# A hybrid encoder layer on one core: the second token group's feature-major products as seven quarter products, the lanes beside token-major blocks, an output block in two depth halves

## The chip, the cores and the metric

The kernel runs on one core of a Trainium2 chip. The metric is device time in microseconds (us), from the first to the last instruction of the core. TensorE (PE) multiplies matrices into PSUM, VectorE (DVE) and ScalarE (ACT) do elementwise work, GpSimd (POOL) does a little of it, and the SyncE queue (SP) issues the transfers.

## The reference, cut to what matters

One encoder layer is applied to 1024 + 256 tokens of width 2048, with shared weights, in fp32. The normalised input is multiplied by `w_in`, and the product's columns go to three groups of heads, whose results are concatenated and multiplied by `w_out`:

```python
proj = rms_norm(x, norm_g) @ w_in                    # 2048 x 4896
xbc, z_ssd, dt_raw, q, k, v, z_att, mq, z_mem = split_cols(proj, IN_SIZES)
xbc = silu(centred_dwconv(xbc, conv_w, conv_b))      # 1536 columns, 5 taps over tokens
o_ssd = rms_norm((scan(xbc, dt) + scan_back(xbc, dt) + skip) * silu(z_ssd))
o_att = window_attention(q, k, v, sink) * silu(z_att)
o_mem = softmax(mq @ mk) @ mv * silu(z_mem)          # mk, mv from the memory tokens
y = x + concat([o_ssd, o_att, o_mem]) @ w_out        # 2048 x 2048
```

## The kernel before, in words

The ten tiles of 128 tokens are two groups of five: tokens 0 to 639 (group one, `grp` 0) and 640 to 1279 (group two, `grp` 1). Every fp32 operand is split into a high part (`h`, ScalarE) and the remainder (`l`, VectorE), so that each product is three matmuls: h·h, h·l, l·h. For weights this is `wsplit` (L200 to L204), one ScalarE and one VectorE instruction per depth step; `wh` and `wl` have three buffers each (`WB`), so weights are split up to three depth steps ahead of TensorE. A group's input rows lie in SBUF as `xH`, `xL` in four quads of four depth steps.

There are three kinds of product blocks.

- `block_tok` (L230): token-major. Sixteen depth steps, each with five token tiles times three matmuls of 512 columns (288 for "kv"). Used for the memory blocks, "q", "kv", "mq", "z0", "z1" and, for the first 640 output tokens, the four output blocks `o`.
- `block_feat` (L264): feature-major. 256 features by 640 tokens in two halves of 320: 2 x 2 x 16 depth steps x 3 = 192 matmuls of 320 columns. Group two uses it for the ten units x0 to x5 (the convolution's input), za0, za1, zm0, zm1 (gates).
- `block_pair` (L1174): the same 256 x 640 unit by seven quarter products of half depth instead of eight, from sums and differences of rows (`tH`, `tL`) and of weights (`weight_sums`, L1154, four POOL instructions per depth step): 7 x 8 x 3 = 168 matmuls of 320 columns. Group one uses it for its ten units, `rows_in` picking the operands; the output for group two uses it at the end (8 units). Its evacuation is `ev_seven` (L1271), whose units' partial sums lie in a tile with the tag `xst`. Statistics (`stage_stats`, L1356) load pieces of the inputs into the same tag.

What follows a convolution unit (five taps, tanh, product: L345 to L379) or a gate unit is put into the queue `left` and issued piece by piece by `some_left`. `p_step` (L1260) builds group one's rows by a written plan: load, scale by the norm (`p_fill`, L1227, with the splits), sums (`p_sums`), splits of the sums (`p_split`).

The rest runs in two **lanes**, queues of generators that are stepped beside the blocks: lane 0 has the key preparation, attention `attn` and memory attention `mem_attn`; lane 1 has the scans' preparation `dt_prep`, `ssd_up` and `ssd_down`. `run` (L1361) calls `pump(rates)` once per depth step; `RATES` gives how many steps of lane 0 and lane 1 fall due then, by block. `need(fn, ts)` steps a lane until the named generators are done. The framework that builds the kernel keeps each lane's order but places an instruction in its engine's order where its inputs are expected, so lane matmuls come to lie between block matmuls.

The order before: two memory blocks and "q" of group one; ten units of quarter products of group one; then, with the lanes beside them, "kv", "mq", "z0", "z1" of group one, x0 to x4, "kv", x5, "q", za0, za1, "z0", "z1", "mq", zm0, zm1 of group two, output blocks o0, o1 and the first nine steps of o2; the rest of o2 and o3 with `beside_step`, which builds the rows of the output's quarter products; those eight units.

All loads and stores are issued by the SP queue.

Of the kernel before, what the change touches and what calls it, by code (L numbers as in the profile page):

```python
# [19 lines left out]
P = 128  # L20
# [23 lines left out]
def hymba_encoder_kernel(  # L44
# [65 lines left out]
    k_d = [dram([P, P], f"k_{t}") for t in range(NT)]  # L110
# [119 lines left out]
    def block_tok(w, nt, evac, before_last=None, feats=range(KT), places=range(KT)):  # L230

        load, n = w
        ps = [acc.tile([P, 512], F32, tag="acc", name="acc") for _ in range(nt)]
        hls = {}
        for k in range(KT):
# [7 lines left out]
            if k == KT - 2:  # L243
                continue
            if k == KT - 1 and before_last is not None:
                before_last(k)

            for t in range(nt):
                for k_ in ((k - 1, k) if k == KT - 1 else (k,)):
# [6 lines left out]
                    T.matmul(ps[t][:, :n], sl, h[:, :n], start=False, stop=(k_ == KT - 1))  # L256
                if k == KT - 1:
                    with tc.high_priority(offset=HP[0]):
                        evac(t, ps[t])
            if k == KT - 1:  # L260
                yield k - 1
# [64 lines left out]
    def ev_dtkv(base):  # L326
        def f(i, ps):
            t = base + i
            r = ev.tile([P, P], F32, tag="evt" if i % 2 else "evu", name="kraw")
            A.activation(r, ps[:, 32:160], AF.Copy)  # L330
            S.dma_start(k_d[t], r)
            V.tensor_add(dt_all[:, t, :], ps[:, :32], dtb)
            V.tensor_copy(v_all[:, i + (2 if base else 0), :], ps[:, 160:288])
        return f
# [63 lines left out]
    def ev_out(c0):  # L398
        def f(t, ps):
# [5 lines left out]
            S.dma_start(yt, xrow(t)[:, c0:c0 + 512])  # L405
            V.tensor_add(yt, ps, yt)
            S.dma_start(y_first[t * P:(t + 1) * P, c0:c0 + 512], yt)
# [68 lines left out]
    def k_prep(t):  # L476
        r = w2("kr")[:, :P]
        S.dma_start(r, k_d[t])
# [8 lines left out]
        r3 = hv(r, 2)  # L487
        V.tensor_mul(r3, r3, hb(rr, 2, 64))
# [19 lines left out]
    def kv_shift():  # L508

        V.tensor_copy(kT[:, :, 0:2 * P], kT[:, :, 3 * P:5 * P].bitcast(F32))  # L510
        V.tensor_copy(kL[:, :, 0:2 * P], kL[:, :, 3 * P:5 * P].bitcast(F32))
        V.tensor_copy(v_all[:, 0:2, :], v_all[:, 3:5, :])

    def dt_prep(t0):
# [6 lines left out]
        x = flat(dt_all)  # L521
        e, s = [mp.tile([P, 512], F32, tag="xs", name=n, bufs=2)[:, :160] for n in "es"]
# [275 lines left out]
    def ssd_up(t):  # L798
# [63 lines left out]
        for g in range(2):  # L862
# [23 lines left out]
            if not last:  # L886
                ps = psum("pst")
                into(ps, g, fh, fl)
                if t == 0 and g == 0:

                    need(mk_prep, range(4))
# [328 lines left out]
    def p_load(k):  # L1220

        raw[k] = [rp.tile([P, 640], F32, tag="ch", name=n, bufs=CH) for n in ("ra", "rb_")]
        for i in range(2):
            r = k + 8 * i
            S.dma_start(raw[k][i], x_turned[0, r * P:(r + 1) * P, :])

    def p_fill(k):  # L1227

        for i, x in enumerate(raw[k]):
            q, j = divmod(k + 8 * i, 4)  # L1230
            if j == 0:
                new_quad(q)
            g_ = R_G + k + 8 * i
            V.scalar_tensor_tensor(out=x, in0=x, scalar=vec[:, g_:g_ + 1], in1=rbc, op0=ALU.mult, op1=ALU.mult)
            h, l = cur["H", q][:, j, :], cur["L", q][:, j, :]
            A.activation(h, x, AF.Copy)
            V.tensor_sub(l, x, h.bitcast(F32))

# [32 lines left out]
    def ev_seven(kind, f0):  # L1271

        work, o = (conv_left, 2) if kind is None else (gate_left, 0)

        def begin(u):
            if kind is None:
                tiles = [rp.tile([P, 650], F32, tag="ch", name="u", bufs=CH) for _ in range(2)]
                for x in tiles:
                    V.memset(x[:, :2], 0.0)
            else:  # L1280
                tiles = [ev.tile([P, 650], F32, tag="evu", name="r") for _ in range(2)]
            r0, r1 = [hv(x[:, o:o + 640], 2) for x in tiles]
            w = None

            def f(p, ps):
# [10 lines left out]
                elif p == 3:  # L1296
                    V.tensor_add(r0[:, 1], ps, w[:, 1])
# [139 lines left out]
    def vectors(_):  # L1437
# [6 lines left out]
        for _ in range(4):  # L1444
            yield
# [235 lines left out]
```

## Time and profile before

| what | value |
|---|---|
| median of three runs | 1803.67 us (1800.71 to 1803.76) |
| the profiled execution: its time | 1800.71 us |
| its span | 1800.7 us |
| granted TensorE clock | 1.000 |
| HBM read, written | 231.12 MB, 57.44 MB |
| 16 DMA engines' share of the first queue | 52.7% |

A row of a stretch gives its bounds, its length, then for each engine the busy time and the number of instructions, the granted clock, the share of the DMA engines and what they moved. A row of a group gives line, engine, operation, tiles and shapes, the count, then busy time in us and the mean duration in ns, then the idle time ahead of it and what ended that. A row in order of time begins with the start and the duration in us.

### The profile page before, as it was taken

How to read it: one execution, taken by the hardware profiler on the slowest of the kernel's cores; microseconds unless marked ns; L12 is line 12 of the kernel's file. 1: busy time of each engine (PE TensorE's matmuls, PEld its weight loads, DVE VectorE, ACT ScalarE, POOL GpSimd, SP SyncE). 2: the span in 40 equal slices, each digit the busy share in tenths (PEclk: the TensorE clock that was granted, in tenths of full speed). 3: DMA queues.
4: the chain of work that ended last, by engine and by line, in shares of the span. 5: the costliest groups of instructions: out<-in, count | busy, mean ns of one | idle time of the engine just before them, and what ended most of it. 6: DMA issues, size and time to landing. Idle time of an engine off the chain costs nothing.

```text
span 1800.7 us, 30423 instructions
## 1 busy us (share of the span) xinstructions
PE 1791.2 (99%) x10546; PEld 1606.1 (89%) x10546; DVE 1244.3 (69%) x2422; ACT 903.0 (50%) x2039; POOL 439.5 (24%) x714
## 2 busy tenths in 40 slices
PE   9999999999999999999999999999999999999999
PEld 7789999999887899999989987887898888889999
DVE  5595788877657978775755866666885654866665
ACT  6554455444445756564435646544574533543332
POOL 0105789961110000000000000001100000058775
PEclk9999999999999999999999999999999999999999
DMA  8664455446544644444436355457785564644442
GB/s 291 198 179 120 138 153 146 129 136 218 164 136 147 184 134 140 121 132 134 119 96 192 110 161 180 128 178 235 231 266 168 184 190 138 216 153 147 142 143 80
DMA packets 198891, 290.58 MB, mean 161 GB/s; under 512 B 18960, under 2 KB 80464, under 8 KB 198736
## 3 DMA queue, kind: packets, MB, share of 16 engines
q1 hardware_dynamic: 198592, 288.57, 52.7%
q8 instruction: 83, 1.36, 0.3%
q14 instruction: 72, 0.59, 0.1%
q10 hardware_dynamic: 144, 0.06, 0.0%
HBM read 231.12 MB, written 57.44 MB: 160 GB/s over the span
## 4 chain that ended last, share of the span: by engine, by line
PE 61%; DVE 1%; ACT 1%; issue 1%; DMA 1%; POOL 0%; POOLq 0%; ACTq 0%; DVEq 0%
PE acc L254 9%; PE acc L256 8%; PE acc L255 8%; PE acc L289 5%; PE acc L291 5%; PE acc L290 5%; PE acc L1199 3%; PE acc L1201 3%; PE acc L1200 3%; PE py L931 2%; PE po L674 1%; PE ppt L664 1%; PE accm L1200 1%; PE accm L1201 1%; PE accm L1199 1%
## 5 line engine op out<-in xcount | busy, mean ns | idle before, releaser
L203 DVE TENSOR_TENSOR wl<-wraw,wh 128x512 fp32r<-128x512 f32 (+1 forms) x480 | 338.9, 708 | 241.3 <-ACT wh L202 230.7
L254 PE MATMUL acc<-wh,xH 128*128 128x512 f32 (+1 forms) x1248 | 481.9, 386 | 0.2 <-ACT mkr L416 0.2
L255 PE MATMUL acc<-wl,xH 128*128 128x512 f32 (+1 forms) x1248 | 472.2, 378 | 0.9 <-DVE wl L203 0.6
L256 PE MATMUL acc<-wh,xL 128*128 128x512 f32 (+1 forms) x1248 | 472.8, 379 | 0.0
L202 ACT ACTIVATE wh<-wraw 128x512 fp32r<-128x512 f32 (+1 forms) x480 | 292.4, 613 | 323.5 <-PE acc L256 173.3
L254 PEld LDWEIGHTS acc<-wh,xH 128*128 128x128 f32 x1248 | 234.5, 188 | 45.1 <-issue 4.8
L255 PEld LDWEIGHTS acc<-wl,xH 128*128 128x128 f32 x1248 | 234.7, 188 | 43.8 <-DVE wl L203 3.3
L256 PEld LDWEIGHTS acc<-wh,xL 128*128 128x128 f32 x1248 | 234.2, 188 | 43.9 <-issue 0.9
L289 PE MATMUL acc<-xH,wh 128*128 128x320 f32 x640 | 204.5, 320 | 0.0
L291 PE MATMUL acc<-xH,wl 128*128 128x320 f32 x640 | 198.6, 310 | 0.0
L290 PE MATMUL acc<-xL,wh 128*128 128x320 f32 x640 | 198.3, 310 | 0.0
L203 DVE TENSOR_TENSOR sl<-ws,sh 128x384 fp32r<-128x384 f32 x144 | 99.6, 695 | 96.9 <-ACT sh L202 96.6
L202 ACT ACTIVATE sh<-ws 128x384 fp32r<-128x384 f32 x144 | 74.6, 523 | 176.5 <-POOL ws L1171 81.5
L1171 POOL TENSOR_TENSOR ws<-wraw 128x128 f32<-128x128 f32 x144 | 91.1, 633 | 202.0 <-DMA wraw<-in_w_in_pairs_dram 83.6
L289 PEld LDWEIGHTS acc<-xH,wh 128*128 128x128 f32 x640 | 120.3, 188 | 4.1 <-issue 3.7
L290 PEld LDWEIGHTS acc<-xL,wh 128*128 128x128 f32 x640 | 120.3, 188 | 2.6 <-issue 2.2
L291 PEld LDWEIGHTS acc<-xH,wl 128*128 128x128 f32 x640 | 120.1, 188 | 0.7 <-issue 0.6
L1171 POOL TENSOR_TENSOR ws<-wraw,ws 128x128 f32<-128x128 f32 x144 | 93.5, 649 | 11.3
L358 DVE SCALAR_TENSOR_TENSOR c<-u,vec,c 128x638 f32<-128x638 f32 (+1 forms) x96 | 88.6, 926 | 10.0 <-ACT c L353 9.7
L1171 POOL TENSOR_TENSOR ws<-ws,wraw 128x128 f32<-128x128 f32 x144 | 94.2, 654 | 0.0
L120 POOL TENSOR_SCALAR qr<-qss 128x8 f32<-128x8 f32 x10 | 4.3, 428 | 366.6 <-DVE qss L598 366.6
L1171 POOL TENSOR_TENSOR wraw<-wraw 128x128 f32<-128x128 f32 x144 | 89.2, 620 | 11.1
(427 smaller groups left out, 3645.1 us busy)
## 6 DMA issues: line engine op xcount, KB each, us to landing
wraw<-in_w_in_laid_dram SPq DMA_DIRECT2D x208, 256.0 KB, 2.8
wraw<-in_w_in_pairs_dram SPq DMA_DIRECT2D x80, 256.0 KB, 2.8
wraw<-in_w_out_laid_dram SPq DMA_DIRECT2D x64, 256.0 KB, 3.5
wraw<-in_w_out_pairs_dram SPq DMA_DIRECT2D x64, 256.0 KB, 2.8
rf<-ac SPq DMA_DIRECT2D x40, 256.0 KB, 3.7
rb<-ac SPq DMA_DIRECT2D x40, 256.0 KB, 4.1
wraw<-in_w_mem_laid_dram SPq DMA_DIRECT2D x32, 256.0 KB, 4.8
xst<-in_x_sample_dram SPq DMA_DIRECT2D x20, 256.0 KB, 4.7
```

The costliest lines, as they stand in the source:

```text
L202: a = A.activation(h, raw, AF.Copy)
L203: b = V.tensor_sub(l, raw, h.bitcast(F32))
L254: T.matmul(ps[t][:, :n], sh, h[:, :n], start=(k_ == 0), stop=False)
L255: T.matmul(ps[t][:, :n], sh, l[:, :n], start=False, stop=False)
L256: T.matmul(ps[t][:, :n], sl, h[:, :n], start=False, stop=(k_ == KT - 1))
L289: T.matmul(o, sh, cur["H", q][:, m, c], start=(k == 0), stop=False)
L290: T.matmul(o, sh, cur["L", q][:, m, c], start=False, stop=False)
L291: T.matmul(o, sl, cur["H", q][:, m, c], start=False, stop=(k == KT - 1))
L358: V.scalar_tensor_tensor(out=c[0], in0=u[:, k:k + n], scalar=cw[k], in1=c[0], op0=ALU.mult, op1=ALU.add)
L1171: G.tensor_tensor(out=o, in0=x, in1=y, op=op)
L1199: T.matmul(ps[p], h, xh, start=(k_ == 0), stop=False)
L1200: T.matmul(ps[p], h, xl, start=False, stop=False)
```

## The change

Group two's ten feature-major units become quarter products too, ahead of the lanes. "kv" and "mq" of group one run before them without lanes, and beside these two blocks `t_step` builds group two's rows; the scaled rows of both groups are kept in DRAM (`xs_d`) and read back. The lanes then run beside seven token-major blocks: "kv", "q", "mq", "z0", "z1" of group two, and, with group one's rows read back, "z0", "z1" of group one. The four token-major output blocks are cut in depth: the first half (attention and memory attention) with the lanes, its sums with `x` added parked in DRAM (`ym_d`); the second half (scans) after it, added to the parked sums. `RATES` are higher, as the lanes have fewer depth steps. "kv" is written to DRAM whole and read back by the lanes. The statistics of tokens 640 to 1279 move ahead, in the first quarter-product stretch, with a fifth step per unit.

```diff
-RATES = ({'kv': (2.0, 1.0), 'mq': (2.4, 1.6), 'z0': (2.2, 1.7), 'z1': (2.2, 1.7)},
-         {'kv': (1.2, 1.5), 'x': (1.75, 1.85), 'q': (1.6, 2.5), 'za': (1.6, 2.5), 'z0': (1.55, 2.6),
-          'z1': (1.55, 2.65), 'mq': (1.55, 2.8), 'zm': (1.55, 2.85), 'o': (1.95, 1.9)})
+RATES = {'kv': (2.0, 2.0), 'q': (3.1, 3.3), 'mq': (3.1, 3.3), 'z1': (3.1, 3.3), 'z0': (3.1, 3.3), 'o': (3.1, 3.6)}
...
-            S.dma_start(yt, xrow(t)[:, c0:c0 + 512])
+            S.dma_start(yt, ym_d[c][t] if part else xrow(t)[:, c0:c0 + 512])
             V.tensor_add(yt, ps, yt)
-            S.dma_start(y_first[t * P:(t + 1) * P, c0:c0 + 512], yt)
+            S.dma_start(y_first[t * P:(t + 1) * P, c0:c0 + 512] if part else ym_d[c][t], yt)
...
+    def p_scale(k, grp=0):
 
         for i, x in enumerate(raw[k]):
+            r = k + 8 * i
+            V.scalar_tensor_tensor(out=x, in0=x, scalar=vec[:, R_G + r:R_G + r + 1], in1=rbc, op0=ALU.mult, op1=ALU.mult)
+            S.dma_start(xs_d[grp][r], x)
...
+    def r_load(k):
+
+        again[k] = [rp.tile([P, 640], F32, tag="ch", name=n, bufs=CH) for n in ("ra", "rb_")]
+        for i in range(2):
+            S.dma_start(again[k][i], xs_d[1][k + 8 * i])
+
+    def r_fill(k):
+        p_rows(k, again.pop(k))
...
+    t_plan = {}
+    for k in range(8):
+        at = (3, 6, 9, 12, 15, 17, 19, 21)[k]
+        for j, f in ((at - 2, lambda k: p_load(k, 1)), (at, lambda k: p_scale(k, 1)), (at + 1, p_sums), (at + 2, p_split)):
+            t_plan.setdefault(j, []).append((f, k))
+    for k, at in enumerate((25, 27, 29, 31, 32, 33, 35, 37)):
+        for j, f in ((at - 2, r_load), (at, r_fill)):
+            t_plan.setdefault(j, []).append((f, k))
...
+    def pairs_in(grp, extra):
+        nonlocal owe
+        for u, unit in enumerate(units):
+            for k in block_pair(w_in_pairs, u, rows_in, ev_seven(*unit, grp), lead=2):
+                if k in (0, 2, 4, 5, 7):
+                    next(squares, None)
...
+    pairs_in(0, p_step)
...
+    run(block_tok(w_in_rows("kv"), 5, ev_dtkv(0)), (0, 0), extra=left_and(t_step))
+    run(block_tok(w_in_rows("mq"), 5, ev_raw(mq_d, 0), feats=PAIRED, places=PAIRED), (0, 0),
+        extra=left_and(lambda k: t_step(16 + k)))
+    pairs_in(1, t_step)
     early.close()
...
+    def first_steps(k):
+        while left and k > 2:
             some_left()
 
+    tok("kv", 1, ev_dtkv(5), extra=first_steps, hold=4)
...
+    tok("q", 1, ev_raw(q_d, 5))
+    tok("mq", 1, ev_raw(mq_d, 5))
+    tok("z0", 1, ev_gate(0, 5))
+    tok("z1", 1, ev_gate(1, 5), refill_x(0))
+    tok("z0", 0, ev_gate(0, 0))
...
+    tok("z1", 0, ev_gate(1, 0), lambda q: refill_o(0)(q) if q < 2 else [])
...
+    for c in range(4):
+        run(block_tok(w_out_rows(c), 5, ev_out(c, 0), feats=range(8), places=range(8)), RATES["o"],
+            (lambda q: refill_o(0)(q + 2)) if c == 2 else None)
+    for c in range(4):
+        j0 = 8 * c - 16
+        rest = range(8, KT)
+        for k in block_tok(w_out_rows(c), 5, ev_out(c, 1), before_last=lambda _: beside_step(j0 + 6), feats=rest, places=rest):
...
             if j0 + k < -7:
-                pump(RATES[1]["o"])
+                pump(RATES["o"])
```

More of the change, by code (lines that the diff above doesn't have):

```diff
@@ L487, in k_prep @@
         r3 = hv(r, 2)
+        need(vectors, [0])
         V.tensor_mul(r3, r3, hb(rr, 2, 64))
@@ L1282, in begin @@
             r0, r1 = [hv(x[:, o:o + 640], 2) for x in tiles]
+            second = ((0, 64, 324), (64, 320, 392)) if kind is None and grp else ((0, 320, o + 320),)
             w = None
@@ L1566, in hymba_encoder_kernel @@
+    queue(0, attn, range(5, 10))
     queue(1, dt_prep, [5])
[L1567 to L1576 removed]
+    queue(1, ssd_up, range(4, 8))
```

229 lines of the change are left out of this document (112 added, 117 removed).

## The prediction, made before the changed kernel was run

> **What bounds the kernel now.** I read the page's busy shares first, then the busy time by stretch, then the order of time of TensorE and VectorE.
>
> ```profile
> span 1800.7 us, 30423 instructions
> PE 1791.2 (99%) x10546; PEld 1606.1 (89%) x10546; DVE 1244.3 (69%) x2422; ACT 903.0 (50%) x2039; POOL 439.5 (24%) x714
> ```
>
> TensorE is idle for 9.5 us of 1800.7. A busy matmul is modelled and may be waiting, so I checked the distance from start to start. Three places follow: the quarter products of the first group, a feature-major block of the second, a token-major block. Each pair of lines is the first and the last of a run of matmuls with nothing else between them.
>
> ```profile
> 379.81 0.31 PE L1201 MATMUL acc<-xH,sl 128*128 128x320 f32 x1
> ...
> 387.99 0.30 PE L1200 MATMUL acc<-tL,sh 128*128 128x320 f32 x1
> ...
> 639.76 0.31 PE L290 MATMUL acc<-xL,wh 128*128 128x320 f32 x1
> ...
> 642.99 0.31 PE L291 MATMUL acc<-xH,wl 128*128 128x320 f32 x1
> ...
> 499.65 0.39 PE L254 MATMUL acc<-wh,xH 128*128 128x512 f32 x1
> ...
> 502.85 0.39 PE L256 MATMUL acc<-wh,xL 128*128 128x512 f32 x1
> ```
>
> 57 matmuls, 23 matmuls and 15 matmuls stand there: 8.18/56 = 0.146 us, 3.23/22 = 0.147 us and 3.20/14 = 0.229 us each. Duration (0.31, 0.39) is not cost; spacing is. VectorE is read the same way; its order of time has a weight split, and what came next:
>
> ```profile
> 607.14 0.68 DVE L203 TENSOR_TENSOR wl<-wraw,wh 128x512 fp32r<-128x512 f32 x1
> 607.74 0.94 DVE L637 TENSOR_REDUCE m<-lg 128x2 f32<-128x768 f32 x1
> ```
>
> The next one starts 0.60 us after a start whose duration is 0.68: 0.08 us of each duration is overlap. Now the stretches: the quarter products of group one, the first "kv", the first "z1", the first "zm" up to the output, block "q" of group one with the building of its rows, and all in which the lanes run.
>
> ```profile
> core 0: us, PE busy (x) PEld busy (x) DVE busy (x) ACT busy (x) POOL busy (x), PEclk, DMA share, GB/s
> 151.90:399.20 247.30, 246.85 (x1681) 245.47 (x1680) 197.00 (x298) 126.25 (x253) 201.95 (x310) 1.00 0.47 138
> 399.20:430.80 31.60, 31.60 (x242) 31.60 (x241) 21.55 (x49) 16.70 (x43) 4.17 (x10) 1.00 0.78 242
> 553.10:632.50 79.40, 79.22 (x410) 62.33 (x408) 72.57 (x165) 54.43 (x142) 3.67 (x4) 1.00 0.55 164
> 1258.70:1335.70 77.00, 76.55 (x518) 70.68 (x517) 64.33 (x151) 45.61 (x116) 6.53 (x14) 1.00 0.81 251
> ...
> 96.80:151.90 55.10, 54.99 (x241) 44.90 (x241) 44.10 (x72) 26.82 (x45) 11.36 (x20) 1.00 0.53 160
> ...
> 399.20:1544.80 1145.60, 1142.75 (x6641) 997.28 (x6640) 784.43 (x1702) 592.87 (x1458) 68.13 (x108) 1.00 0.54 164
> ```
>
> The reader is to see two things. The 1680 matmuls of the quarter products take 247.3 us, 0.147 us each, so that stretch has no slack to lose or to win. And in the lane stretch the granted clock is 1.00 and VectorE is busy 0.68 of the time, but 0.91 in "z1" (72.57 of 79.40) while TensorE misses 0.18 us. TensorE bounds every stretch; only fewer matmuls shorten it.
>
> **The change, part by part.**
>
> **Fewer products.** These rows of the page go.
>
> ```profile
> L289 PE MATMUL acc<-xH,wh 128*128 128x320 f32 x640 | 204.5, 320 | 0.0
> L291 PE MATMUL acc<-xH,wl 128*128 128x320 f32 x640 | 198.6, 310 | 0.0
> L290 PE MATMUL acc<-xL,wh 128*128 128x320 f32 x640 | 198.3, 310 | 0.0
> ```
>
> 1920 matmuls leave, 1680 come (ten units of seven products, eight depth steps, three matmuls): 240 fewer at 0.147 us is **-35.3 us**. All other matmuls keep their number and width; the output block in halves has 8 x 5 x 3 twice instead of 16 x 5 x 3 once.
>
> **The second quarter-product stretch.** It repeats 151.90:399.20 with the same POOL sums. The convolution taps come with it. They cost more beside POOL than in the lane stretch, by the mean:
>
> ```profile
> L358 DVE SCALAR_TENSOR_TENSOR c<-u,vec,c 128x638 f32<-128x638 f32 x37 | 36.6, 991 | 0.1
> ```
>
> against 887 ns (row below). But the first stretch carried these very taps with TensorE 246.85 of 247.30 busy, so I take 0; if the cover went, the 48 taps' 0.1 us each are 5 us.
>
> In the first stretch a wait is added: the statistics get a fifth step per unit and their pieces share one buffer (`xst`) with the units' sums, so that in seven of ten units a piece is alive when the sums begin. Behind the first sum stand the unit's six others on VectorE, and the next unit's first product needs the bank.
>
> ```profile
> xst<-in_x_sample_dram SPq DMA_DIRECT2D x20, 256.0 KB, 4.7
> ```
>
> A piece that starts only then lands 4.7 us later; the 42 matmuls of the last two depth steps take 6.1 us. It fits by a little; I take 0, with 7 x 1 us as the other end.
>
> **Rows of group two, built beside "kv" and "mq".** Without lanes, the matmuls there take 31.6 + 54.5 = 86 us. The same work for group one has these prices:
>
> ```profile
> L1234 DVE SCALAR_TENSOR_TENSOR ra<-ra,vec,rbc 128x640 f32<-128x640 f32 x8 | 7.0, 879 | 0.0
> L1237 DVE TENSOR_TENSOR xL<-ra,xH 128x640 fp32r<-128x640 f32 x8 | 6.5, 818 | 0.0
> L1243 DVE TENSOR_TENSOR ra<-ra 128x320 f32<-128x320 f32 x8 | 4.1, 517 | 0.0
> ```
>
> 16 scalings, 32 subtractions and 24 splits of rows (eight more fall into the first product unit), 14 left-over taps, 16 narrow and 16 wide weight splits (0.458 and 0.688, rows below), each less the 0.08: 13 + 14 + 18 + 11 + 6 + 10 = 72 us of 86, a share of 0.84. Block "q" did such work at 44.10 of 55.10, 0.80, and TensorE missed 0.11 us. I take 0; should the cover fail, it is the 3 us or so by which 0.84 exceeds 0.80. The 48 added transfers of 0.33 MB are 16 MB, spread over "kv", "mq", "q" and the block ahead of it, some 190 us: 84 GB/s on top of the 160 of "q" is less than the 251 of "zm", so 0 for them too.
>
> **The lane stretch.** The two lanes (attention, memory attention, state scans) move from 1145.6 us to behind the second product stretch, beside seven token-major blocks and the output halves. TensorE first. Of the 1145.6 us, the wide token-major blocks are 10 x 240 x 0.227, "kv" 2 x 240 x 0.132, the feature-major ones 1920 x 0.147: 545 + 63 + 282 = 890. (0.227 is what most pairs of neighbours show, 54.5 us per block and within 1% of the 0.229 above; 0.132 is 31.60/240.) The rest, 255 us and some, is the lanes' own matmuls with every wait in it. Afterwards: one "kv" 32, six blocks 327, four half blocks 109, nine steps of 15 matmuls 31, and the same 255: **754 us**. The rates drain the lanes there: 12 steps at 2.0, 96 at 3.1, 41 at 3.1 make 449 for lane 0, whose generators have 442 steps; 24 + 96 x 3.3 + 41 x 3.6 = 488 for lane 1 with 487. The scans that the third half block's refill needs are step 396, and 409 are then done. So nothing is forced at the end.
>
> VectorE next. What leaves its 784.4 us, with the rows:
>
> ```profile
> L203 DVE TENSOR_TENSOR wl<-wraw,wh 128x512 fp32r<-128x512 f32 x241 | 165.6, 688 | 163.8 <-ACT wh L202 154.7 <-DMA rb<-ac 3.5 <-DMA xc<-xbc_d 2.7
> L358 DVE SCALAR_TENSOR_TENSOR c<-u,vec,c 128x646 f32<-128x646 f32 x48 | 42.3, 887 | 9.8 <-ACT c L353 9.7
> L203 DVE TENSOR_TENSOR wl<-wraw,wh 128x288 fp32r<-128x288 f32 x31 | 14.2, 458 | 23.9 <-ACT wh L202 23.9
> L190 DVE SCALAR_TENSOR_TENSOR chd<-chd,vec,rbc 128x640 f32<-128x640 f32 x16 | 13.8, 880 | 0.4 <-DMA chd<-in_x_turned_dram 0.4
> L364 DVE SCALAR_TENSOR_TENSOR u<-u,c 128x646 f32<-128x646 f32 x12 | 9.9, 827 | 0.2 <-ACT u L361 0.2
> L358 DVE SCALAR_TENSOR_TENSOR c<-u,vec,c 128x638 f32<-128x638 f32 x11 | 9.7, 879 | 0.1
> L406 DVE TENSOR_TENSOR yt<-acc,yt 128x512 f32<-128x512 f32 x14 | 9.5, 686 | 2.2 <-PE acc L256 2.1
> L315 DVE SCALAR_TENSOR_TENSOR zs<-zs,acc 128x320 f32<-128x320 f32 x16 | 7.4, 484 | 5.1 <-ACT zs L314 5.1
> ...
> L202 ACT ACTIVATE wh<-wraw 128x512 fp32r<-128x512 f32 (+1 forms) x480 | 292.4, 613 | 323.5 <-PE acc L256 173.3
> ```
>
> 104 wide splits of 0.688 (137 of 241 stay), 15 narrow ones, 48 taps and 12 last steps, 16 scalings, 16 gate products: 71.6 + 6.9 + 52.2 + 13.8 + 7.4 = 152. Eleven more output additions of 0.686 come: +8. So 784 - 152 + 8 = **640 us in 754, a share of 0.85**, below the 0.91 that "z1" bears with 0.18 us of TensorE idle. ScalarE has 593 less 104 splits of 0.61 (the last row), some 530 of 754. Transfers: 164 GB/s x 1145.6 us = 188 MB, less 104 x 0.26 MB and with 5 MB of parked halves 166 MB, 220 GB/s; "zm" had 251. None is over a level that the trace shows without loss.
>
> **The price of density.** The trace has no place with 6.4 lane steps in a depth step; "z1" has 3.9 in 79.40/16 = 5.0 us. What a lane's wait costs is seen there: a score matmul, the end of its softmax, and its transposes.
>
> ```profile
> 600.80 0.41 PE L632 MATMUL psc<-kT,qT 128*128 128x384 f32 x1
> ...
> 610.01 0.74 DVE L652 TENSOR_SCALAR lg<-lg,den 128x384 f32<-128x384 f32 x2
> ...
> 610.48 0.88 PE L664 MATMUL ppt<-identr,lg 128*128 128x128 f32 x6
> ```
>
> The chain lasts 9.7 us and TensorE fills it with block matmuls: the transposes stand in its order where their input is ready, between two matmuls of one triple. So density alone costs near nothing as long as block matmuls are at hand. The dearest known spot is the start: 14 left-over convolution steps are issued at once in the fourth step of "kv" (11 taps of 0.88 and 3 last steps of about 0.82, less the 0.08: 11 us of VectorE), while TensorE has split weights for three steps of 31.60/16 = 2.0 us. 11 - 6 is 5 us; with 1 us for four more block changes **+6**. Its ends are 0 (the same left-overs beside the first "kv", one per step, cost nothing: 31.60 busy of 31.60) and 19, the whole burst with the 1 us and the 7 us of the statistics.
>
> **Sum.** 1800.7 - 35.3 + 6 = 1771.4 for the profiled execution. It was the fastest of the three runs shown, its time 1800.71 being its span; the median is 3.0 higher: **1774 us**.
>
> **Rivals.**
>
> **VectorE becomes the bound.** I took 0.08 us of each duration as overlap. If each instruction held the engine for all of it, the 640 us would grow by 0.08 for each of some 1702 - 200 instructions: 120 us, 760 in all, more than TensorE's 754. With no idle time that is +6; with the 0.09 that VectorE still idles in "z1" it is 760/0.91 = 835, +81. The start-to-start row lies at the lower end, so I take +35 of this band, from its lower half: 1800.7 - 35.3 + 35 + 3 = 1803, no change. The spacing row speaks against it. [...]
>
> **TensorE waits at the lanes' turns (slower).** Place: the 40 groups of transposes of attention and the 20 of memory attention. Score and transpose are three lane-0 steps apart; at 3.1 steps in 754/149 = 5.1 us that is 4.9 us against a chain of 9.7. If the order cannot put enough block matmuls between, because only three depth steps of weights are split ahead, each group waits. Longest waits now:
>
> ```profile
> PE pmt L759 <- DVE mpr L751: 1.3, 2, 0.8
> PE ppt L664 <- DVE lg L652: 0.9, 2, 0.5
> ```
>
> It decides from 35.3/60 = 0.6 us per group; at 0.8 it is 48 us: 1800.7 - 35.3 + 48 + 3 = 1816. For it speaks the density, against it that these four waits came to 2.2 us in the whole stretch.
>
> **The saving is not there**, because the product stretch is bound by something else: excluded by 0.147 us per matmul in both forms.
>
> **How the numbers follow.** Forecast 1774, its own band 1762 to 1790: 0.64. VectorE bound, 1790 to 1810: 0.18. Waits at the turns, 1807 to 1850: 0.15. Better than 1762: 0.03. This kernel's measurement tells 0.2% (3.6 us) from no change, so "same" is 1800 to 1807. Of the second case I put 0.06 below, 0.08 in and 0.04 above it: faster 0.73, same 0.08, slower 0.19. The range 1762 to 1806 leaves out 0.03 below and some 0.17 above.
>
> **What would show it.** Right: 1680 more matmuls on the lines of the quarter products (4704 with the output's) and none on the feature-major lines; two stretches of about 247 us; a lane stretch of 754 to 765 us with VectorE busy 0.83 to 0.87 and the waits of TensorE under 10 us in all; "kv" of group two near 37 us plus its lane matmuls. Wrong: VectorE over 0.95 there and TensorE's matmuls waiting for `wl`; or waits of `ppt` and `pmt` of over 30 us; or a second product stretch over 255 us.

## The result, and the profile after

The changed kernel takes **1825.92 us** (median of 4, 1822.18 to 1831.61), the kernel before 1802.34 us (1800.71 to 1803.76): a ratio of **1.0136 [1.0121, 1.0152]**, slower by 24 us where the prediction had it faster by 30. The profiled execution after took 1827.37 us with a span of 1825.6.

The head of the page of after, the same two lines that the prediction quotes of before:

```profile
span 1825.6 us, 31134 instructions
PE 1779.5 (97%) x10306; PEld 1575.4 (86%) x10306; DVE 1394.0 (76%) x2638; ACT 952.9 (52%) x2117; POOL 654.1 (36%) x1034
```

10306 matmuls against 10546: the 240 are gone. But TensorE is now idle for 46.1 us (1825.6 - 1779.5), before for 9.5. Where that is, the busy times by stretch of after show: "q" of group one; the first quarter products; "kv" and "mq" of group one, with group two's rows built beside them; the second quarter products; all the rest up to the end of the second closing half block, with the lanes.

```profile
core 0: us, PE busy (x) PEld busy (x) DVE busy (x) ACT busy (x) POOL busy (x), PEclk, DMA share, GB/s
98.40:159.20 60.80, 56.89 (x242) 45.81 (x240) 45.80 (x75) 27.60 (x46) 10.96 (x20) 0.97 0.63 213
159.20:413.50 254.30, 249.41 (x1690) 246.54 (x1689) 196.91 (x303) 131.65 (x269) 201.88 (x314) 1.00 0.46 142
413.50:509.00 95.50, 90.39 (x484) 78.29 (x483) 77.52 (x125) 40.35 (x70) 17.11 (x24) 0.96 0.77 252
509.00:755.60 246.60, 245.78 (x1681) 245.40 (x1680) 205.02 (x331) 116.69 (x205) 198.39 (x296) 1.00 0.36 112
755.60:1569.30 813.70, 790.26 (x4230) 640.22 (x4229) 649.92 (x1454) 481.08 (x1244) 68.63 (x104) 0.99 0.62 196
```

Against what the same work took or should take:

| Stretch | after, us | basis, us | excess |
|---|---|---|---|
| start of the kernel to the first quarter product | 159.2 | 151.9 (before) | 7.3 |
| first quarter products | 254.3 | 247.3 (before) | 7.0 |
| "kv", "mq" of group one | 95.5 | 86.3 (31.6 and 54.5, and the change of block) | 9.2 |
| second quarter products | 246.6 | 247.3 (forecast) | -0.7 |
| lane stretch | 813.7 | 777.8 | 35.9 |

The basis of the last row is the forecast's 754 us with the seven steps of the second closing half block that it left out, 7 x 15 x 0.227 = 23.8. The excesses add up to 58.7 us (59.4 less the 0.7), of which the forecast had 6. The saving of 35 us is there, and more than one and a half times as much is spent. In the lane stretch 23.4 us of the 35.9 are idle time of TensorE (813.70 - 790.26); 6.8 us more are its clock, shown below, and the other 5.7 us stand in no row of idle time. VectorE is busy 649.9 us, 0.80, not at its limit (682.7 us in 816.15, 0.84, in a run below). In "kv" and "mq" 5.1 us of the 9.2 are idle time, and 3.4 the clock.

The waits of TensorE in that stretch of after (engine, what it wanted, who ended the wait, then us in total, times, longest):

```profile
PE ppt L674 <- DVE lg L662: 7.2, 3, 3.4
PE pms L747 <- ACT mqh L732: 3.2, 2, 2.7
PE pacs L563 <- DVE w L552: 2.7, 2, 1.4
PE pst L867 <- ACT fh L881: 1.5, 3, 0.8
PE acc L255 <- ACT wh L202: 1.3, 1, 1.3
PE pst L867 <- ACT bh L894: 1.3, 1, 1.3
```

No place stands out: 23 waits in all, most for a lane's own data, two (2.0 us) for a block's weights. The longest can be followed. First the load that it began with, in the view of the tile `yd` between 1276 and 1283 us: its data was stored by `ssd_up` from 1273.0 on, the load was issued at 1276.5 and landed 5.1 us later, at 1281.6.

```profile
L1018 SPq DMA_DIRECT2D yd<-yp x1: 326/326/326, 1276.5 to 1276.5; - x1
...
DMA to landing us min/median/max: 5.1/5.1/5.1
```

Then the order of time of after around it, VectorE, ScalarE and TensorE (start, duration, engine, instruction, in brackets the idle time before it and what ended that):

```profile
1278.53 0.15 DVE L650 TENSOR_TENSOR m<-m,sinkb 128x2 f32<-128x2 f32 x1
1281.74 0.69 DVE L1040 TENSOR_TENSOR yd<-yd,zd 128x512 f32<-128x512 f32 x1 [3.05 <-issue]
1282.35 0.16 DVE L651 TENSOR_SCALAR nm<-m 128x2 f32<-128x2 f32 x1
...
1282.47 0.63 ACT L1041 ACTIVATE zd<-yd 128x512 f32<-128x512 f32 x1 [6.91 <-DVE yd L1040]
...
1283.19 0.60 ACT L657 ACTIVATE lg<-lg,nm 128x384 f32<-128x384 f32 x1
...
1282.92 0.39 PE L255 MATMUL acc<-wh,xH 128*128 128x512 f32 x1
1286.73 1.05 PE L674 MATMUL ppt<-identr,lg 128*128 128x128 f32 x6 [3.42 <-DVE lg L662]
1287.43 0.67 PE L642 MATMUL psc<-kT,qT 128*128 128x384 f32 x1
```

Read it from the top. A product of lane 1 waits 3.05 us on VectorE; the profile names no releaser (`issue`), but the product starts as the load lands. Behind it stands `nm` of lane 0's softmax, whose input was there at 1278.7 and which runs at 1282.35: VectorE ran its instructions in their order. Behind `nm` on ScalarE are the exponentials, which also stand behind lane 1's square. (VectorE then waits another 1.02 us for lane 1's `yrs`, ahead of the softmax's `den`.) The transposes of that softmax stand in TensorE's order ahead of the other 14 matmuls of the block's depth step, whose weights were split by 1275.8: these could have run. A lane that is late for 3 us thus stops the other lane and then TensorE for 3.4 us. And it doesn't end there; the busy times of after in the 3.35 us that follow:

```profile
1287.35:1290.70 3.35, 3.35 (x12) 2.96 (x11) 1.86 (x6) 1.91 (x6) 0.00 (x0) 0.50 0.74 233
```

The granted clock is 0.50, and block matmuls of 512 columns start 0.43 us apart in place of 0.227. Before had no such window in its span; in the lane stretch of after there are four of 3.4 us, each behind 3.4 us in which TensorE was idle for 2.0 to 2.9, which costs another 4 x 1.7 = 6.8 us.

### The profile page after: what moved, and what is told of

Its sections match the earlier page's. It is cut to its first block, busy times and chain, and to the rows that moved or that the text cites. A ratio compares the mean times of both kernels' runs of the same rounds, so it can differ in the third digit from the quotient of the medians.

```text
span 1825.6 us, 31134 instructions
## 1 busy us (share of the span) xinstructions
PE 1779.5 (97%) x10306; PEld 1575.4 (86%) x10306; DVE 1394.0 (76%) x2638; ACT 952.9 (52%) x2117; POOL 654.1 (36%) x1034
## 4 chain that ended last, share of the span: by engine, by line
PE 73%; DMA 9%; issue 7%; DVE 6%; POOL 3%; ACT 2%; SPq 0%; ACTq 0%; POOLq 0%; DVEq 0%
PE acc L256 9%; PE acc L257 9%; PE acc L255 9%; PE acc L1208 8%; PE acc L1206 8%; PE acc L1207 8%; PE accm L1207 3%; PE accm L1206 3%; PE accm L1208 3%; PE py L938 2%; POOL ws L1178 1%; DVE wl L203 1%; PE po L684 1%; PE ppt L674 1%; PE pyb L1036 1%
## 5 line engine op out<-in xcount | busy, mean ns | idle before, releaser
L1178 POOL TENSOR_TENSOR ws<-wraw,ws 128x128 f32<-128x128 f32 x224 | 150.7, 673 | 17.3
L1178 POOL TENSOR_TENSOR ws<-ws,wraw 128x128 f32<-128x128 f32 x224 | 151.4, 676 | 0.0
L1208 PE MATMUL acc<-xH,wl 128*128 128x320 f32 x320 | 98.9, 309 | 3.2 <-DVE wl L203 3.2
L1206 PE MATMUL acc<-xH,wh 128*128 128x320 f32 x320 | 99.1, 310 | 1.7 <-ACT wh L202 1.7
L1207 PE MATMUL accm<-tL,wh 128*128 128x320 f32 x320 | 99.0, 310 | 0.0
L1206 PE MATMUL accm<-tH,wh 128*128 128x320 f32 x320 | 99.0, 309 | 0.0
L1208 PE MATMUL acc<-tH,sl 128*128 128x320 f32 x320 | 98.9, 309 | 0.0
L1207 PE MATMUL acc<-xL,wh 128*128 128x320 f32 x320 | 98.7, 308 | 0.0
L1206 PE MATMUL acc<-tH,sh 128*128 128x320 f32 x320 | 98.6, 308 | 0.0
L1208 PE MATMUL accm<-tH,wl 128*128 128x320 f32 x320 | 98.5, 308 | 0.0
```

The costliest lines, as they stand in the source:

```text
L1178: G.tensor_tensor(out=o, in0=x, in1=y, op=op)
L1206: T.matmul(ps[p], h, xh, start=(k_ == 0), stop=False)
L1207: T.matmul(ps[p], h, xl, start=False, stop=False)
L1208: T.matmul(ps[p], l, xh, start=False, stop=(k_ == 7))
```

## The experiments

Two theories at the start. **Density**: the lanes' chains are as long as before, but there are fewer block matmuls to put between their steps, and engines that run their instructions in order, as VectorE did above, pass each delay on. **VectorE**: more work per us on it makes it the bound, the prediction's first rival. Each stretch with an excess then got its own runs. Where kernels were profiled again with a stretch untouched, its length moved: "q" 58 to 63 us, the first quarter products 251 to 258, the lane stretch 814 to 818.

### VectorE with more work, and with less

More: a clearing of 320 columns of `rbc`, which nothing reads any more, at each of 149 depth steps. (A tile of its own to clear did not fit into SBUF: 57 kb of a partition, where 56.1 are left.)

```
     def pump(rates):
+
+        if more:
+            with ExitStack() as st:
+                for ins in marks:
+                    st.enter_context(tc.issue_after(ins))
+                V.memset(rbc[:, :320], 0.0)
```

> The changed kernel with one more VectorE instruction per step of the lanes' pump (149 clearings of 320 columns of a tile that is no longer used, 0.2 to 0.35 us each, 30 to 50 us in all), for which nothing waits. VectorE's throughput as the bound: the lane stretch of 814 to 820 us grows by most of what is added. The fixed order with its waits: VectorE's idle time takes most of it and the stretch grows by less than a third of it. The run that took 47 us off VectorE made the stretch no shorter, so I expect the second.

Less: the scalings of both softmaxes and the copy of `xs` go to ScalarE; a doubling of `den` takes over the factor 0.5.

```
+            V.tensor_scalar(out=den, in0=den, scalar1=2.0, scalar2=None, op0=ALU.mult)
...
-                V.tensor_scalar(out=lg[:, kv, :nk], in0=lg[:, kv, :nk], scalar1=den[:, kv:kv + 1], scalar2=0.5,
-                                op0=ALU.mult, op1=ALU.mult)
+                A.activation(lg[:, kv, :nk], lg[:, kv, :nk], AF.Copy, scale=den[:, kv:kv + 1])
...
-            V.tensor_copy(xt, ps)
+            A.activation(xt, ps, AF.Copy)
```

> The changed kernel with 140 instructions of the lanes moved from VectorE to ScalarE (the scaling of both attentions' weights, the copies of the scans' transposed rows), about 47 us off VectorE, 5 us of small ones added to it, and some 50 us on ScalarE, which is busy 0.6 there. If VectorE's throughput makes the lane stretch 36 us longer than TensorE's work, the stretch goes from 814 us to 775 to 785 and the whole to about 1790. If it is waits from a fixed order whose steps now follow each other too closely, VectorE has capacity to spare and the stretch changes by less than 10 us either way.

Measured: with more 1832.29 us, 1.0169 [1.0142, 1.0196]; with less 1835.06 us, 1.0182 [1.0164, 1.0201]. The busy times of the lane stretch, with more:

```profile
753.22:1569.37 816.15, 789.76 (x4230) 639.00 (x4229) 682.69 (x1603) 484.07 (x1244) 69.67 (x104) 0.99 0.63 195
```

and with less:

```profile
756.19:1576.39 820.20, 791.88 (x4231) 636.60 (x4229) 612.00 (x1374) 542.11 (x1384) 66.56 (x104) 1.00 0.63 194
```

VectorE busy for 683 or 612 us in place of 650 gives 816 or 820 in place of 814; by their medians the two kernels are 6.4 and 9.1 us over the changed one. A bound on VectorE would have given 33 us more and 38 less. The VectorE theory falls. That the lighter one is slightly the longer fits engines in order (work moved onto ScalarE stands ahead of the `wh` splits there), which this run alone doesn't show.

### Three blocks in place of one in the first part

```
+    tok("z0", 1, ev_gate(0, 5))
     tok("mq", 1, ev_raw(mq_d, 5))
+    tok("z0", 1, ev_gate(0, 5))
```

with the rates of that part at 2.21 and 2.36 in place of 3.1 and 3.3.

> The changed kernel with the block z0 of group two computed three times instead of once, and the lanes' rates in the first part of the lane stretch (q to the late z0) lowered from 3.1 and 3.3 to 2.21 and 2.36, so that the same lane steps stand at 0.85 of a step per us instead of 1.1. The rest of the stretch (late z1 and output halves) keeps its rates and is the control. 480 matmuls of 0.227 us add 109 us, so the first part would go from 421 to 530 us with the same waits. If the waits come from lane steps that follow too closely, it takes 514 to 520 us and TensorE's idle time there, 6 us now, goes below 2, while the control keeps its 352 us and its idle time of about 14 us. If the waits belong to single events (transfers, evictions), the first part takes 530.

Measured 1926.17 us. From "q" to "z0" of group one 524.3 us in place of 421.3 + 109 = 530.3, idle 2.5 in place of 6.0; the late part, with unchanged rates, 345.9 in place of 352.1. Three tenths less density brought 6 us there, but the late part moved by as much without an edit. It points to density and settles nothing.

### The lanes at the density of before

So the density went down to that of the kernel before: six token-major blocks ("z0" of each group three more times) and four half blocks more, the rates halved.

```
-RATES = {'kv': (2.0, 2.0), 'q': (3.1, 3.3), 'mq': (3.1, 3.3), 'z1': (3.1, 3.3), 'z0': (3.1, 3.3), 'o': (3.1, 3.6)}
+RATES = {'kv': (2.0, 2.0), 'q': (1.55, 1.65), 'mq': (1.55, 1.65), 'z1': (1.55, 1.65), 'z0': (1.55, 1.65), 'o': (1.74, 2.03)}
...
-    for c in range(4):
+    for c in (0, 1, 0, 1, 0, 1, 2, 3):
```

> Six token-major blocks and four half blocks of the output are computed a second or third time (the same values stored again), spread over the lane stretch, and the lanes' rates there are halved, so that the lanes run about as dense as in the kernel before. The added matmuls are 6 x 54.5 + 4 x 27.2 = 436 us. Theory, density: the 36 us by which the lane stretch of the changed kernel exceeds the sum of its matmuls (TensorE idle 23 us, half-clock windows behind it) fall to 10 or less; the stretch is 814 + 436 - 26 to 36 = 1214 to 1224 us, and the granted clock stays at full speed there. Rival, the loss sits in single places (new order of the lanes, half blocks, refills) whatever the density: the idle time stays at 18 us or more, and the stretch is 1240 to 1255 us.

Measured 2230.61 us; the lane stretch and all its longer waits of TensorE:

```profile
752.95:1972.81 1219.86, 1213.30 (x6151) 997.11 (x6149) 780.38 (x1632) 581.48 (x1402) 64.69 (x104) 1.00 0.57 174
```

```profile
PE pacs L563 <- DVE w L552: 1.9, 1, 1.9
PE acc L256 <- DVE wl L203: 1.7, 2, 0.9
PE acc L255 <- ACT wh L202: 1.3, 2, 1.1
PE pms L749 <- DVE mql L734: 0.8, 1, 0.8
```

1219.9 - 436 = 783.9 us: the excess over 777.8 falls **from 36 to 6 us**, the idle time from 23.4 to 6.6, of which 5.0 lie in "kv" of group two, whose rates weren't changed. The granted clock is 1.00. The same lanes, refills and half blocks in the same order lose nearly nothing when the block matmuls beside them take 959 us (523 + 436) in place of 523. The load on VectorE fell too, from 0.80 to 0.64, but the runs before this one rule it out. Slower transfers are no rival either: the lanes' loads landed after the same time (medians before, after and here: `rb` 4.1, 3.9, 4.2 us; `xc` 4.5, 3.6, 3.5; `yd` 3.3, 3.7, 3.7). Density it is, 30 of the 36 us.

How it works, the order of time tells for the 40 softmax chains of attention, from the second score matmul (L643; L633 before) to the end of the scaling (L662; L652). Their median is 8.7 us before and 8.7 after (7.6 in this run): the chains became no longer. The distance from that end to the first transpose (L674; L664) changed: a median of 0.92 us before, 0.03 after, 3.87 in this run; under 0.3 us in 14, 28 and 8 of the 40. Before, most transposes came to an input that lay ready. After, TensorE arrives when the input does, so that each delay on the way is one of TensorE.

### Two single late places mended

`pause` is a generator of six empty steps; it stands ahead of both sequences of `ssd_down`, and lane 1's rates are raised for it ("z1" 3.45, "o" 3.8). The left-over convolution steps are issued two to a depth step.

```
+    queue(1, pause, [0])
     queue(1, ssd_down, range(7, -1, -1))
...
-        while left and k > 2:
-            some_left()
+        for _ in range(2):
+            if left:
+                some_left()
```

> Two edits of order in the lane stretch: six empty steps stand ahead of each of the two sequences of the scans' way down (which read back what the last step of the way up has just stored), with lane 1's rate raised for them in the last blocks; and the left-over convolution steps are issued two to a depth step of kv of group two, not all in its fourth step. If single late inputs make the loss: the waits of 3.0 to 3.4 us for ppt at 1287 us and 1383 us and the half-clock windows behind them go, and kv of group two falls from 40 to 36 us, in all 10 to 15 us less. Rival, density: other waits take their place, and the stretch stays within 4 us of 814.

Measured 1832.51 us, 1.0166 [1.0134, 1.0197]; its lane stretch:

```profile
756.83:1581.55 824.72, 792.88 (x4230) 641.04 (x4229) 649.39 (x1452) 481.73 (x1244) 68.23 (x104) 0.99 0.63 192
```

The waits for `ppt` fell from 7.2 to 2.9 us, and others came: one of 3.6 us for `psc`, one of 3.4 for `pmt`, one of 2.9 for `pst`. "kv" of group two took 40.9 us, no less. The stretch is 11 us longer in this profile, which is of the slowest of the four executions; by the medians the kernel is 6.6 us over the changed one. At this density a wait that is mended is replaced.

### The low halves of the weight splits on POOL

```
-        b = V.tensor_sub(l, raw, h.bitcast(F32))
+        b = low[0].tensor_sub(l, raw, h.bitcast(F32))
...
+    low[0] = G
...
+    low[0] = V
```

in the token-major blocks beside the lanes and after them.

> The low halves of the weight splits of the 137 token-major depth steps beside the lanes are taken from VectorE to POOL, which is busy 0.08 there; ScalarE keeps the high halves. Theory A, engines that take their instructions in order: a weight split stands on VectorE behind a lane instruction that waits for a transfer or for another engine, and TensorE waits for the split. Then the waits of TensorE for wl from VectorE (7.4 + 3.2 us and others, some 11 us) go, VectorE is freed of 137 x 0.6 = 82 us, the lanes' chains get shorter too, and the lane stretch falls from 814 us by 10 to 25 us; what stays are the waits for ppt, pms and pacs. Rival B, the lanes' own inputs come late whatever the splits do: the stretch stays within 5 us of 814. Rival C, POOL is too slow for a split: TensorE waits for wl from POOL, and the stretch grows.

Measured 1897.66 us, 1.053 [1.0508, 1.0551]. The group of these splits, the waits of TensorE in the lane stretch, and that stretch:

```profile
L205 POOL TENSOR_TENSOR wl<-wraw,wh 128x512 fp32r<-128x512 f32 (+1 forms) x176 | 236.2, 1345 | 527.0 <-ACT wh L204 495.3 <-DMA rb<-ac 10.5 <-PE acc L259 5.3
```

```profile
PE ppt L676 <- DVE lg L664: 14.2, 14, 3.1
PE pst L870 <- DVE bl L909: 7.0, 5, 2.5
PE pmt L771 <- DVE mpr L763: 6.4, 8, 1.1
```

```profile
758.25:1631.70 873.45, 810.65 (x4231) 648.47 (x4229) 631.27 (x1289) 483.11 (x1244) 275.54 (x264) 0.98 0.59 181
```

None of the three theories of the expectation: not A, the stretch grew by 60 us; not quite C, since TensorE waited for the lanes (`ppt` 14 times in place of 3), not for `wl`. Idle time is 62.8 us with VectorE at 0.72. Why splits on another engine make the lanes' data so much later stays open; that it isn't VectorE's load is shown once more.

### The first quarter products

Three runs. The prediction feared the buffer that statistics and sums share. A buffer of its own for the pieces doesn't fit into SBUF (98 kb of a partition, where 97.7 are left). With groups of four pieces and steps 0, 1, 2, 4, 5 no piece is alive when the sums begin:

```
-                         lambda i: fin.tile([P, 512], F32, tag="xst", name="sst"), ahead=1, group=3)
+                         lambda i: fin.tile([P, 512], F32, tag="xst", name="sst"), ahead=1, group=4)
...
-                if k in (0, 2, 4, 5, 7):
+                if k in (0, 1, 2, 4, 5):
```

> The changed kernel with the statistics in groups of four pieces and their five steps at depth steps 0, 1, 2, 4, 5 of a unit, so that a group begins and ends inside one unit and no piece is alive when the unit's sums take the shared buffer. If that buffer costs the first quarter-product stretch its 7 us (254 to 258 us in three profiles, 247.3 before), the stretch goes to 247 to 250 us and the whole to about 1818 to 1820. If the loss comes from ScalarE waiting for the pieces' landing, which stays, the stretch remains at 252 or more.

Measured 1834.55 us, 1.0174 [1.0156, 1.0192]; the stretch 256.9 us in place of 254.3. The buffer is not it. Next, the stores of the scaled rows, left out for group one; the late refill then reads group two's rows, so two gate blocks of group one compute from those:

```
+            if grp:
                 S.dma_start(xs_d[grp][r], x)
```

> The changed kernel without the 16 stores of group one's scaled rows; the refill for the two late gate blocks reads group two's rows instead, so those two blocks compute with the wrong rows. If these stores are what makes the start longer (7.3 us up to the first product unit: the sums are made in place and wait for the store, and the loads of weights stand behind the stores in the SP queue), the first product unit begins near 153 us instead of 159.2, and the whole is 5 to 8 us shorter than the changed kernel's 1826. If something else in the start does it, the first unit still begins at 158 to 160 and the time stays within 2 us of 1826. Either way the lane stretch keeps its 814 us.

Measured 1827.11 us, 1.0137 [1.0119, 1.0156]: "q" 57.2 us in place of 60.8, the stretch 257.6. The stores cost nothing after "q". What they cost "q" isn't shown: 57.2 us is the shortest of these profiles, but with the stores "q" took from 57.7 to 63.4, and TensorE's waits for `wl` there are 2.2 us with and without them. Last, the memory tiles' statistics beside the second quarter products, with four steps per unit:

```
-    squares = stage_stats()
+    squares = stage_stats([(xrow(t), t) for t in range(5, 10)])
...
-                if k in (0, 2, 4, 5, 7):
+                if k in (0, 2, 4, 5):
...
+    squares = stage_stats([(mrow(i), 10 + i) for i in range(4)])
     pairs_in(1, t_step)
```

> The 16 squares of the four memory tiles' statistics are moved from the first product stretch to the second, four in a unit there; the first keeps the 20 of rows 5 to 9, in four steps of a unit as the kernel before had them. Theory: ScalarE takes its instructions in order, a square waits for its piece (41 us in 24 waits in the first stretch), and the splits behind it are late; with fewer pieces the first stretch falls from 254 to 247 to 249 us, and the second rises by 0 to 3. Rival: the stretch is longer for the stores and transfers left over from the start, or for another reason: it stays at 254 or more.

Measured 1821.52 us, 1.0116 [1.0075, 1.0157]. Its four stretches from the first quarter products on:

```profile
159.26:406.59 247.33, 247.21 (x1691) 246.53 (x1690) 200.09 (x299) 121.92 (x237) 199.76 (x306) 1.00 0.44 128
406.59:501.48 94.89, 90.12 (x484) 77.21 (x482) 77.67 (x125) 40.10 (x70) 16.52 (x24) 0.98 0.77 252
501.48:748.63 247.15, 245.73 (x1681) 245.47 (x1680) 208.26 (x335) 124.45 (x237) 203.97 (x304) 1.00 0.42 129
748.63:1564.78 816.15, 788.25 (x4231) 637.23 (x4229) 648.91 (x1454) 481.26 (x1244) 68.69 (x104) 1.00 0.64 195
```

254.3 becomes 247.3 (247.2 in the next run with the same edit), the idle time 0.1, and the second stretch rises by 0.5. So the added statistics are the cause: in the kernel before this stretch had 28 squares in four steps per unit, after it has 36 in five (the pieces of tokens 1024 to 1279 came), here 20 in four. In after TensorE waits there for the weight splits, 3.2 us for `wl` and 1.7 for `wh`. ScalarE waits for pieces of the statistics to land; in after there are four such rows, 24 waits of 40.5 us:

```profile
ACT sst L1392 <- DMA sst<-in_mem_sample_dram: 12.8, 6, 3.6
ACT sst L1392 <- DMA sst<-in_mem_prompt_dram: 11.9, 8, 3.0
ACT sst L1392 <- DMA sst<-in_x_sample_dram: 8.4, 4, 3.5
ACT sst L1392 <- DMA sst<-in_x_prompt_dram: 7.4, 6, 3.1
```

in this run two, 12 waits of 17.4 us:

```profile
ACT sst L1392 <- DMA sst<-in_x_sample_dram: 11.5, 6, 3.9
...
ACT sst L1392 <- DMA sst<-in_x_prompt_dram: 5.9, 6, 2.0
```

and in the kernel before three, 20 waits of 36.0 us:

```profile
ACT sst L1336 <- DMA sst<-in_x_sample_dram: 18.3, 9, 4.6
ACT sst L1336 <- DMA sst<-in_mem_prompt_dram: 9.7, 5, 2.5
ACT sst L1336 <- DMA sst<-in_mem_sample_dram: 8.0, 6, 4.2
```

One of them, in after: a square waits 2.02 us on ScalarE for its piece, up to 303.29 us, the `sh` and `wh` splits behind it start at 303.92 and 304.34, and TensorE waits 0.88 us for that `wh`, up to 305.00. But the kernel before had nearly as much of this and took 247.3 us, so the sum of these waits is not the price. Four such steps per unit fit, five don't; why the fifth tips it was only argued.

### Group two's rows beside "kv" and "mq"

First the weights: those of the first two depth steps of the quarter products were loaded and summed six steps sooner, for both stretches (with the statistics as in the last run).

```
-            if j in (27, 29):
-                weight_sums(w_in_pairs, (j - 27) // 2)
+            if j in (21, 23):
+                weight_sums(w_in_pairs, (j - 21) // 2)
```

> The memory tiles' statistics beside the second quarter products (as in the run before that did this alone), and the first two depth steps' weights of each quarter-product stretch are loaded and summed six steps sooner, in q and in mq of group one. Theory: ScalarE waits at the split of the weight sums for POOL, which waits for the weights' transfer (9 us in three waits at the end of mq, one of 4 us at the end of q), the splits of the running block stand behind it, and TensorE waits for these; sooner sums take that away: q 61 to 57 or 58 us, kv and mq 95 to 90 or 92 us, no other stretch changed, in all 5 to 9 us less than with the statistics alone (1821.5 us). Rival, VectorE's load there (busy 0.81) or the stores set the time: these stretches stay within 2 us.

Measured 1820.23 us, 1.0091 [1.0075, 1.0108]. "q" 59.4 us in place of 62.1 in the run before, "kv" and "mq" 94.2 in place of 94.9: this theory falls for the second place, and for the first the change is within what "q" moves by itself. Then the same test as for the lanes, more block beside the same work: "mq" twice, the sums spread over the three blocks.

```
-        at = (3, 6, 9, 12, 15, 17, 19, 21)[k]
+        at = (5, 9, 14, 18, 23, 26, 29, 32)[k]
...
+    run(block_tok(w_in_rows("mq"), 5, ev_raw(mq_d, 0), feats=PAIRED, places=PAIRED), (0, 0),
+        extra=left_and(lambda k: t_step(32 + k)))
```

> Block mq of group one is computed twice in a row (the same values stored again), and the scalings, sums and their splits for group two's rows are spread over the three blocks (first to last from step 5 to 34 in place of 3 to 23); the reading back of the rows keeps its pace of one pair in two steps, in the last of the three, since it overwrites rows that this block still reads. The added matmuls are 54.5 us. Theory, density of the row building (VectorE 0.81 there): the 9 us by which kv and mq of group one exceed their matmuls' 86.3 us fall to 4 or less, the stretch is 141 to 145 us. Rival, the loss sits in the reading back and the first weight sums at the end of mq: the first two blocks lose under 2 us, the last one 5 us or more, and the stretch is 147 to 151 us.

Measured 1875.61 us; the three blocks:

```profile
411.72:555.56 143.84, 141.72 (x724) 121.66 (x722) 87.56 (x141) 53.84 (x93) 14.70 (x24) 1.00 0.64 206
```

143.8 - 54.5 = 89.3: the excess falls from 9.2 to 3.0 us, and the last block, where the rows are read back at the old pace, loses 0.9 of it. Density again, of VectorE's work on the rows and what waits for it in order; the granted clock is 1.00 here, 0.96 in after.

### The output halves alone

The kernel before with its output block one in halves, the sums parked and added, nothing else.

```
+    for c in range(4):
+        run(block_tok(w_out_rows(c), 5, ev_out(c, 0), feats=range(8), places=range(8)), RATES[1]["o"])
...
```

> The kernel before with one part of the change alone: the token-major output block in two depth halves, the first sums parked in DRAM. 20 more additions and 40 more transfers. If the halves cost nothing by themselves, 1800 to 1805 us. If their additional block changes and evictions make TensorE wait, 1808 or more, and the two rows of output halves show it.

Measured 1804.3 us over 10 runs, 1.0012 [1.0003, 1.0022]: at most some 2 us, at the density of before. In its profile these 2 us stand ahead of the first quarter product (153.8 in place of 151.9), where nothing was changed.

No run came out under the kernel before; the lowest of the full work, with the statistics moved and the weights sooner, is 1820.23 us.

## Why the prediction was wrong

**Fewer products: right.** 240 matmuls fewer, and the second stretch with 1680 takes 246.6 us, 0.147 us each.

**The second quarter products: right.** 0 added, -0.7 measured; the tap's dearer price beside POOL was covered.

**The first quarter products: the size was at the upper end, by luck; the reason was wrong.** I took 0 with 7 x 1 us as the other end, for a buffer that came free late. It is 7.0 us (3.7 to 10.8 in the profiles with this stretch unchanged), but not the buffer: it is the fifth step of statistics per unit, whose square stands on ScalarE ahead of splits. I asked only where the piece is stored, not what is queued behind the instruction that waits for it.

**Rows of group two: wrong.** "I take 0", 3 us if the cover failed; it is 9. VectorE's share was 77.5 of 95.5, 0.81, as reckoned (0.84). The step that failed is that a share of 0.80 in one block that lost nothing makes 0.84 safe in the next. With more block beside the same rows 6 of the 9 us went.

**The start: 7.3 us that the forecast put at nothing, cause open.** "q" has 5.7 of them (3.9 idle, 1.7 the clock); it was longer than the 55.1 us of before in every changed kernel, also without the stores (57.2). I priced the added transfers by their bytes. The stores also hold the rows that VectorE then sums in place: it waits 2.7 us for them there. That this reached TensorE isn't shown. The other 1.6 us lie ahead of "q", within what these blocks move by themselves.

**The lane stretch.** TensorE's 754 us of matmuls and VectorE's 640 us (649.9 measured, with the seven further steps) were right, and so was that VectorE isn't the bound. The step that failed is **"density alone costs near nothing as long as block matmuls are at hand"**: the price of density was put at 6 us, 5 of them for a burst in "kv" of group two, and is 36, of which 30 go when the block matmuls are given back. I took that from a stretch with 3.9 steps per depth step; at 6.4 the matmuls weren't at hand any more. The rival that TensorE waits at the lanes' turns had its direction right and its time near (1816 us), by luck, with its place wrong: the transposes of both attentions waited 7.9 us in all (7.2 for `ppt`, 0.7 for `pmt`); the scans, the preparations and the clock took the rest. I gave it 0.15 because four such waits came to 2.2 us before. That number was no evidence for twice the density; the slack of 0.92 us behind it would have been a warning, and I hadn't measured it.

Four errors, then, all of one sign: costs put at or near nothing because a less loaded place hid them. Their sum, 7.3 + 7.0 + 9.2 + 29.9 - 0.7 = 52.7, is the 54.2 us between the sum of 1771.4 and the span of 1825.6, but for 1.5.

## What to carry to other kernels

Here the lanes beside TensorE cost next to nothing while their inputs lay ready before the engine came to them (a median slack of 0.92 us before, with 2.9 us of TensorE idle in the 1145.6 us of the lane stretch), and no longer when they didn't (0.03 us after, with 23.4 us idle in 813.7). So measure that slack, the distance from the end of each chain to its consumer, and not only the waits or the busy shares. Where a change takes matmuls away and leaves the same chains to be hidden, the slack can shrink with them, and a late load can then pass through to TensorE, as the one that landed at 1281.6 us did: VectorE and ScalarE ran their instructions in order, and TensorE waited 3.42 us. To tell density from order, repeat blocks beside the same side work: here 30 of the 36 us vanished with the lanes, 6 of the 9 with the rows, and these were density.

## What the runs showed of the hardware

**In these runs a wait cost more than its length.** The wait of 3.42 us at 1283.31 us of after was followed by 3.4 us at a granted clock of 0.50, another 1.7 us. In the fourteen profiles the granted clock changed only on a grid of 3.413 us, and it followed TensorE's idle time in the stretch of that grid just ended, added up (from the matmul records, whose ends are modelled). Behind a stretch at full clock with less than 1.2 us idle the clock never halved (0 of 7391; in after 0 of 515), with 1.2 to 2 us in 29 of 102 (in after 1 of 4), with more than 2 us in all 31 of 31 (in after 5 of 5). Of the 60 windows at half clock 45 lasted 3.4 us and 15 twice that. Several short waits in one stretch counted together (14 windows followed a stretch without a single wait of 1.2 us), and 11 waits of over 2 us, one of them of 3.34, went free; the grid cut them all in two.

**POOL's price for a split.** A subtraction of 128x512 took 1.389 us there (mean of 160 in the run with the splits on POOL; the row above mixes in 16 of 288 columns), against 0.688 on VectorE in the lane stretch of before.
